# Encoder FFN: four seven-product pairs in the first gate/up block of each later pass, silu as one function, sums in place

## The chip, the cores and the metric

The kernel runs on one core of a Trainium2 chip. The metric is device time in microseconds (us) of one execution. Engines are named as in the profile: PE (matrix), DVE (vector), ACT (scalar), POOL, SP (issues the weight transfers).

## The reference, cut to what matters

A two-layer encoder trunk on 256 rows of width 2048, float32; hidden width of the FFN 5632 (11 blocks of 512). What the change touches is the FFN of both layers:

```python
def swiglu(h, w_gate, w_up, w_down):
    return (jax.nn.silu(h @ w_gate) * (h @ w_up)) @ w_down

for l in range(DEPTH):
    hn = rms_norm(h, mix_norm[l])
    ...
    hn = rms_norm(h, ffn_norm[l])
    h = h + swiglu(hn, ffn_w_gate[l], ffn_w_up[l], ffn_w_down[l])
```

## The kernel before

Every float32 operand is split into a high and a low part, and one product of a 128x128 tile of activations with a 128x512 tile of weights is three matmuls, called h, l and x here: high times high (L301 before, L308 after), high times low of the weights (L302; L309), low of the activations times high (L303; L310).

The hidden columns go in 11 blocks j a layer, 512 gate and 512 up columns each, named f0_j and f1_j by layer. They are taken in passes of blocks 0-1, 2-4, 5-7 and 8-10. After each pass, `stream` computes the down projection of what the pass produced (tiles f0d, f1d), output by output, and adds each output to the residual h on DVE (L283, `residual`). "First block" means blocks 2, 5 and 8, the first of each later pass: three a layer, six in all.

`gate_up` computes one block. It walks over the 16 tiles of 128 rows of the weights as eight pairs p = 0..7. A pair is one 1 MB transfer into `raw` (SP's queue), which holds four 128x512 tiles: gate and up, two rows of tiles each. ACT casts `raw` to `whi`, DVE makes `wlo` = `raw` - `whi` (L324). There are two `wlo` buffers, so `wlo` of pair p cannot begin before PE has read the last of `wlo` of pair p-2. A pair of kind N is eight products, 24 matmuls. A pair of kind S is a seven-product scheme, 21 matmuls, for which DVE forms four sums of the weight tiles (L320 to L322, into `t`), ACT casts them to `thi` (L323) and DVE makes `tlo` (L326); only three of the four plain tiles are then needed, so its `wlo` has 1536 columns. Products of S are P1 to P7, each accumulated in a bank of its own; P6, P7, P4 and P5 use the sums, P1, P2, P3 the plain tiles. Block 0 is plain: N only, with four banks (192 matmuls). The other blocks follow `PAIRS`, a letter for each pair: "NSNSNSNN", 5 x 24 + 3 x 21 = 183 matmuls.

The activation side of a product comes from `x`, or, for P3 of N and most of S, from differences that `make_combos` forms once a layer. A block ends with the gate's silu and the product with up. Eight transposes on PE, which prepare the down projection, lie in every block but the first of a pass.

Inside an engine, instructions run in the order that a scheduler wrote down from priorities. It may therefore let the h matmuls of several products run first, and their l and x later.

Of the kernel before, what the change touches and what calls it, by code (L numbers as in the profile page):

```python
# [72 lines left out]
def trunk(ctx: ExitStack, tc: tile.TileContext, ins, out):  # L73
# [219 lines left out]
    def gate_up(l, j, xs, combos, fx, name, plain, after):
        pattern = "N" * 8 if plain else PAIRS
        bk = [bank("mm", [P, NB], f"{name}_ps{i}") for i in range(4 if plain else 7)]
        uses = {"S": [P1, P2, P3, P6, P7, P4, P5], "N": [0, 1, 2, 3] if plain else [P2, P4, P5, P3]}
# [9 lines left out]
        for p in range(8):  # L306
            raw = wpool.tile([P, 4, NB], F32, tag="raw", name=f"{name}_raw{p}")
# [27 lines left out]
            def w(i):  # L335
                return whi[:, i], wlo[:, i]
# [6 lines left out]
            elif fast:  # L343
# [9 lines left out]
                product(P6, p, sums(1), tw(2), True)
                product(P7, p, sums(3), tw(1), True)
                product(P4, p, x(1, 1), tw(3), True)
                product(P5, p, sums(0), tw(0), True)
            else:
# [666 lines left out]
```

## Time and profile before

| what | value |
|---|---|
| device time, three runs | 2414.62, 2415.92 (median), 2416.74 us |
| profiled execution: its time, its span | 2416.76 us, 2415.0 us |
| PE busy | 2397.6 us, 99% of the span |
| DVE busy, ACT busy | 1744.3 us (72%), 1142.3 us (47%) |
| granted TensorE clock | 1.00 over the FFN blocks (the higher level, 2.4 GHz) |
| bytes moved | 445.50 MB, mean 184 GB/s |

PE is all but never idle: a change of time has to come from fewer matmuls, from the small holes between matmuls, or from new waits of PE. Ends of matmuls are modelled in the profile, so holes are read from their starts. All trace times below are of the profiled execution.

### The profile page before, as it was taken

To read this page: it belongs to the slowest core of one execution; us is meant where nothing else is said; L and a number is where in the kernel's file an instruction comes from. 1 tells how busy PE (TensorE), PEld (TensorE's weight loads), DVE (VectorE), ACT (ScalarE), POOL (GpSimd) and SP (SyncE) were. 2 spreads that over 40 slices of the span, in tenths; PEclk is the share of its full clock that TensorE was granted. 3 is DMA by queue.
4 is the path that set the end of the run, shared out by engine and by line. 5 is a ranking of instruction groups with operands and counts; after the bars stand their busy time and mean duration, and the time that the engine had idled before them with its cause. 6 is when DMAs were issued, how large, how long until landed. Compare 5 with 4: busy or idle time off the path is not lost.

```text
span 2415.0 us, 27558 instructions
## 1 busy us (share of the span) xinstructions
PE 2397.6 (99%) x11212; PEld 1989.3 (82%) x11212; DVE 1744.3 (72%) x1688; ACT 1142.3 (47%) x1056; POOL 54.7 (2%) x63
## 2 busy tenths in 40 slices
PE   8999999999999999999999999999999999999998
PEld 7888888888888888888888888888888888888887
DVE  5658767688678678754768595855878867876884
ACT  5445455455345444454444444454544544544453
...
GB/s 274 161 171 157 174 185 184 197 200 195 192 199 194 196 194 189 209 184 191 165 149 157 157 144 157 153 159 190 191 193 192 196 193 205 186 197 194 205 209 140
DMA packets 63951, 445.50 MB, mean 184 GB/s; under 512 B 6992, under 2 KB 8272, under 8 KB 10576
## 3 DMA queue, kind: packets, MB, share of 16 engines
...
q14 instruction: 39, 0.32, 0.0%
HBM read 441.61 MB, written 2.10 MB: 184 GB/s over the span
## 4 chain that ended last, share of the span: by engine, by line
PE 96%; DVE 2%; DMA 1%; ACT 0%; issue 0%; SPq 0%; ACTq 0%; POOLq 0%; DVEq 0%
PE f_ps L302 12%; PE f_ps L303 12%; PE f_ps L301 12%; PE f1d_ps L166 3%; PE f1d_ps L164 3%; PE f1d_ps L165 3%; PE f0d_ps L166 3%; PE f0d_ps L164 3%; PE f0d_ps L165 3%; PE c_f_ps L165 2%; PE c_f_ps L164 2%; PE c_f_ps L166 2%; PE s_l L765 2%; PE c_i_ps L164 1%; PE c_g_ps L164 1%; PE c_g_ps L166 1%
## 5 line engine op out<-in xcount | busy, mean ns | idle before, releaser
L314 ACT CAST f_whi<-f_raw 128x2048 fp32r<-128x2048 f32 (+1 forms) x176 | 311.2, 1768 | 240.5 <-PE f_ps L303 143.1
L324 DVE TENSOR_TENSOR f_wlo<-f_raw,f_whi 128x2048 fp32r<-128x2048 f32 (+1 forms) x176 | 368.6, 2105 | 43.4 <-PE f_ps L302 32.3
L301 PE MATMUL f_ps<-f_whi,f_x 128*128 128x512 f32 x848 | 331.3, 393 | 0.0
L302 PE MATMUL f_ps<-f_wlo,f_x 128*128 128x512 f32 x848 | 330.2, 389 | 0.9 <-DVE f_wlo L324 0.9
L303 PE MATMUL f_ps<-f_whi,f_x 128*128 128x512 f32 x848 | 330.3, 390 | 0.0
L303 PEld LDWEIGHTS f_ps<-f_whi,f_x 128*128 128x128 f32 x848 | 159.1, 188 | 33.6
L302 PEld LDWEIGHTS f_ps<-f_wlo,f_x 128*128 128x128 f32 x848 | 159.3, 188 | 33.4 <-DVE f_wlo L324 1.3
L301 PEld LDWEIGHTS f_ps<-f_whi,f_x 128*128 128x128 f32 x848 | 159.3, 188 | 32.1
L326 DVE TENSOR_TENSOR f_tlo<-f_t,f_thi 128x2048 fp32r<-128x2048 f32 x60 | 137.3, 2288 | 63.3 <-ACT f_thi L323 63.3
L323 ACT CAST f_thi<-f_t 128x2048 fp32r<-128x2048 f32 x60 | 114.8, 1913 | 134.2 <-DVE f_t L322 108.6
L149 ACT CAST f1d__whi<-f1d__raw 128x2048 fp32r<-128x2048 f32 x44 | 84.4, 1919 | 128.8 <-PE f1d_ps L166 97.5
L150 DVE TENSOR_TENSOR f1d__wlo<-f1d__raw,f1d__whi 128x2048 fp32r<-128x2048 f32 x44 | 100.7, 2289 | 60.6 <-PE f1d_ps L165 32.6
L150 DVE TENSOR_TENSOR f0d__wlo<-f0d__raw,f0d__whi 128x2048 fp32r<-128x2048 f32 x44 | 100.7, 2289 | 59.0 <-PE f0d_ps L165 29.3
L149 ACT CAST f0d__whi<-f0d__raw 128x2048 fp32r<-128x2048 f32 x44 | 84.4, 1918 | 122.1 <-PE f0d_ps L166 91.3
L150 DVE TENSOR_TENSOR c_f_wlo<-c_f_raw,c_f_whi 128x2048 fp32r<-128x2048 f32 x32 | 73.3, 2292 | 72.1 <-PE c_f_ps L165 51.0
L164 PE MATMUL c_f_ps<-c_f_whi,c_x 128*128 128x512 f32 x256 | 101.9, 398 | 0.0
L302 PE MATMUL f_ps<-f_wlo,x_c 128*128 128x512 f32 x260 | 101.1, 389 | 0.0
L303 PE MATMUL f_ps<-f_whi,x_c 128*128 128x512 f32 x260 | 101.1, 389 | 0.0
L301 PE MATMUL f_ps<-f_whi,x_c 128*128 128x512 f32 x260 | 101.1, 389 | 0.0
L165 PE MATMUL c_f_ps<-c_f_wlo,c_x 128*128 128x512 f32 x256 | 99.7, 390 | 0.0
L166 PE MATMUL c_f_ps<-c_f_whi,c_x 128*128 128x512 f32 x256 | 99.7, 389 | 0.0
L149 ACT CAST c_f_whi<-c_f_raw 128x2048 fp32r<-128x2048 f32 x32 | 61.2, 1913 | 76.8 <-PE c_f_ps L166 57.0
...
## 6 DMA issues: line engine op xcount, KB each, us to landing
...
```

The source lines that it names most:

```text
L149: nc.scalar.copy(whi[:, d], raw[:, d])
L150: nc.vector.tensor_tensor(wlo[:, d], raw[:, d], whi[:, d].bitcast(F32), op=ALU.subtract)
L164: nc.tensor.matmul(ps[b], xh[:, k, sl], hi[:, k, :], start=first, stop=False)
L165: nc.tensor.matmul(ps[b], xh[:, k, sl], lo[:, k, :], start=False, stop=False)
L166: nc.tensor.matmul(ps[b], xl[:, k, sl], hi[:, k, :], start=False, stop=end)
L301: nc.tensor.matmul(bk[b], xh, hi, start=b not in seen, stop=False)
L302: nc.tensor.matmul(bk[b], xh, lo, start=False, stop=False)
L303: nc.tensor.matmul(bk[b], xl, hi, start=False, stop=end and final[b] == p)
L314: nc.scalar.copy(whi[:, d], raw[:, d])
L323: nc.scalar.copy(thi, t)
L324: nc.vector.tensor_tensor(wlo[:, d], raw[:, d], whi[:, d].bitcast(F32), op=ALU.subtract)
L326: nc.vector.tensor_tensor(tlo, t, thi.bitcast(F32), op=ALU.subtract)
```

## The change

- `PAIRS` becomes "NNSNSNSN": the three S pairs are 2, 4 and 6 where they were 1, 3 and 5. First blocks follow a new pattern `FIRST`, "SNSNSNSN": four S pairs, 4 x 24 + 4 x 21 = 180 matmuls. Pair 0, with which a block begins, is one of them.
- The sums are formed in place in `raw`, after `wlo` has been made from it (before: into `t`, ahead of `wlo`). The `t` buffer goes. The products of an S pair are called in another order, P1, P6, P7, P2, P4, P5, P3, with the sums in other places.
- `raw` gets four buffers (the pool's three before).
- silu is one ACT function in place of a sigmoid on ACT and a DVE multiply (L411).
- `make_combos` keeps a fifth difference for pairs that are S in one pattern and N in the other, and takes its scratch from the buffer of `thi`.

```diff
-    PAIRS = "NSNSNSNN"
+    PAIRS = "NNSNSNSN"
+    FIRST = "SNSNSNSN"
+    BOTH = "".join(a if a == b else "B" for a, b in zip(PAIRS, FIRST))
...
-        uses = {"S": [P1, P2, P3, P6, P7, P4, P5], "N": [0, 1, 2, 3] if plain else [P2, P4, P5, P3]}
+        uses = {"S": [P1, P6, P7, P2, P4, P5, P3], "N": [0, 1, 2, 3] if plain else [P2, P4, P5, P3]}
...
-            raw = wpool.tile([P, 4, NB], F32, tag="raw", name=f"{name}_raw{p}")
+            raw = wpool.tile([P, 4, NB], F32, tag="raw", name=f"{name}_raw{p}", bufs=RAW_BUFS)
...
                 if fast:
-                    t = fx.tile([P, 4, NB], F32, tag="t", name=f"{name}_t{p}")
                     thi = fx.tile([P, 4, NB], F32R, tag="thi", name=f"{name}_thi{p}")
                     tlo = fx.tile([P, 4, NB], F32R, tag="tlo", name=f"{name}_tlo{p}")
-                    nc.vector.tensor_tensor(t[:, 0:2], raw[:, 0:3:2], raw[:, 3:4].broadcast_to([P, 2, NB]), op=ALU.add)
-                    nc.vector.tensor_tensor(t[:, 2], t[:, 0], raw[:, 2], op=ALU.add)
-                    nc.vector.tensor_tensor(t[:, 3], t[:, 2], raw[:, 1], op=ALU.add)
-                    nc.scalar.copy(thi, t)
                 nc.vector.tensor_tensor(wlo[:, d], raw[:, d], whi[:, d].bitcast(F32), op=ALU.subtract)
                 if fast:
-                    nc.vector.tensor_tensor(tlo, t, thi.bitcast(F32), op=ALU.subtract)
+                    nc.vector.tensor_tensor(raw[:, 2:4], raw[:, 2:4], _ap(raw, 3 * NB, [[-3 * NB, 2], [1, NB]]), op=ALU.add)
+                    nc.vector.tensor_tensor(raw[:, 0], raw[:, 0], raw[:, 2], op=ALU.add)
+                    nc.vector.tensor_tensor(raw[:, 1], raw[:, 0], raw[:, 1], op=ALU.add)
+                    nc.scalar.copy(thi, raw)
+                    nc.vector.tensor_tensor(tlo, raw, thi.bitcast(F32), op=ALU.subtract)
...
-                sg = fx.tile([P, NB], F32, tag="u", name=f"{n}_s{b}", bufs=3)
-                nc.scalar.activation(sg, src, AF.Sigmoid, scale=r(b))
-                nc.vector.scalar_tensor_tensor(out=g, in0=src, scalar=r(b), in1=sg, op0=ALU.mult, op1=ALU.mult)
+                nc.scalar.activation(g, src, AF.Silu, scale=r(b))
...
+                    pattern = None if plain else FIRST if j == blocks[0] else PAIRS
```

What the scheduler makes of it is seen at the start of a first block. On PE, block 5 of layer 0 began with pair 0 as N; the last number in a name is the tile's, banks 4989 to 4995 are P1 to P7, and 4997 and 4998 are `whi` and `wlo` of pair 0:

```order
L301 MATMUL f_5_ps_4990<-f_5_whi_4997,f_x 128x512 [waits Activation_49]
L302 MATMUL f_5_ps_4990<-f_5_wlo_4998,f_x 128x512 [waits DVE_49]
L303 MATMUL f_5_ps_4990<-f_5_whi_4997,f_x 128x512
L301 MATMUL f_5_ps_4990<-f_5_whi_4997,f_x 128x512
L302 MATMUL f_5_ps_4990<-f_5_wlo_4998,f_x 128x512
L303 MATMUL f_5_ps_4990<-f_5_whi_4997,f_x 128x512
```

Now it begins with pair 0 as S (banks 4964 to 4970 are P1 to P7; `whi`, `wlo`, `thi`, `tlo` of pair 0 are 4972, 4973, 4976, 4977; `wlo` of pair 1 is 5007):

```order
L308 MATMUL f_5_ps_4964<-f_5_whi_4972,f_x 128x512 [waits Activation_49]
L309 MATMUL f_5_ps_4964<-f_5_wlo_4973,f_x 128x512 [waits DVE_49]
L310 MATMUL f_5_ps_4964<-f_5_whi_4972,f_x 128x512
L308 MATMUL f_5_ps_4969<-f_5_thi_4976,x_c_2814 128x512 [waits Activation_49]
L308 MATMUL f_5_ps_4970<-f_5_thi_4976,x_c_2814 128x512
L308 MATMUL f_5_ps_4965<-f_5_whi_4972,f_x 128x512
L309 MATMUL f_5_ps_4965<-f_5_wlo_4973,f_x 128x512
L310 MATMUL f_5_ps_4965<-f_5_whi_4972,f_x 128x512
L308 MATMUL f_5_ps_4967<-f_5_thi_4976,f_x 128x512
L308 MATMUL f_5_ps_4968<-f_5_thi_4976,x_c_2814 128x512 [waits DVE_49]
L308 MATMUL f_5_ps_4965<-f_5_whi_5006,f_x 128x512
L309 MATMUL f_5_ps_4965<-f_5_wlo_5007,f_x 128x512 [waits DVE_49]
```

The fourth matmul of the block now reads `thi`, where 24 matmuls in a row read only `whi` and `wlo` of pair 0. Eighteen matmuls into the block, PE reads `tlo` of pair 0, and only behind these eight does P3 read `wlo` of pair 0 for the last time (bank 4966):

```order
L309 MATMUL f_5_ps_4969<-f_5_tlo_4977,x_c_2814 128x512 [waits DVE_49]
L310 MATMUL f_5_ps_4969<-f_5_thi_4976,x_c_2815 128x512
L309 MATMUL f_5_ps_4970<-f_5_tlo_4977,x_c_2814 128x512
L310 MATMUL f_5_ps_4970<-f_5_thi_4976,x_c_2815 128x512
L309 MATMUL f_5_ps_4967<-f_5_tlo_4977,f_x 128x512
L310 MATMUL f_5_ps_4967<-f_5_thi_4976,f_x 128x512
L309 MATMUL f_5_ps_4968<-f_5_tlo_4977,x_c_2814 128x512
L310 MATMUL f_5_ps_4968<-f_5_thi_4976,x_c_2815 128x512
L308 MATMUL f_5_ps_4966<-f_5_whi_4972,x_c_2814 128x512 [waits DVE_49]
L309 MATMUL f_5_ps_4966<-f_5_wlo_4973,x_c_2814 128x512
```

On DVE, the rows ahead of the same block were these (`t` 5031 holds the sums of pair 1, 4957 is the last `wlo` of the down projection, `h_252` the residual):

```order
L150 TENSOR_TENSOR f0d__wlo_4957<-f0d__raw_4955,f0d__whi_4956 128x2048 [waits DVE_49,DMAHW2_49,PE_49,Activation_49]
L320 TENSOR_TENSOR f_5_t_5031<-f_5_raw_5026 128x1024 [waits DMAHW4_49]
L321 TENSOR_TENSOR f_5_t_5031<-f_5_t_5031,f_5_raw_5026 128x512 [waits DVE_49]
L322 TENSOR_TENSOR f_5_t_5031<-f_5_t_5031,f_5_raw_5026 128x512 [waits DVE_49]
L324 TENSOR_TENSOR f_5_wlo_4998<-f_5_raw_4996,f_5_whi_4997 128x2048 [waits DMAHW3_49,PE_49,Activation_49]
L326 TENSOR_TENSOR f_5_tlo_5033<-f_5_t_5031,f_5_thi_5032 128x2048 [waits Activation_49]
L283 TENSOR_TENSOR h_252<-f0d_3_ps_4893,h_252 128x512 [waits PE_49]
L324 TENSOR_TENSOR f_5_wlo_5028<-f_5_raw_5026,f_5_whi_5027 128x1536 [waits PE_49,Activation_49]
L320 TENSOR_TENSOR f_5_t_5096<-f_5_raw_5091 128x1024 [waits DMAHW6_49,DVE_49]
L283 TENSOR_TENSOR h_252<-f0d_3_ps_4894,h_252 128x512 [waits PE_49]
```

They are now (4973 and 4971 are `wlo` and `raw` of pair 0, 5007 and 5037 are `wlo` of pairs 1 and 2):

```order
L151 TENSOR_TENSOR f0d__wlo_4932<-f0d__raw_4930,f0d__whi_4931 128x2048 [waits DVE_49,DMAHW2_49,PE_49,Activation_49]
L325 TENSOR_TENSOR f_5_wlo_4973<-f_5_raw_4971,f_5_whi_4972 128x1536 [waits DVE_49,DMAHW3_49,PE_49,Activation_49]
L328 TENSOR_TENSOR f_5_raw_4971<-f_5_raw_4971 128x1024 [waits DVE_49]
L329 TENSOR_TENSOR f_5_raw_4971<-f_5_raw_4971 128x512 [waits DVE_49]
L330 TENSOR_TENSOR f_5_raw_4971<-f_5_raw_4971 128x512 [waits DVE_49]
L284 TENSOR_TENSOR h_252<-f0d_3_ps_4868,h_252 128x512 [waits PE_49]
L325 TENSOR_TENSOR f_5_wlo_5007<-f_5_raw_5005,f_5_whi_5006 128x2048 [waits DMAHW4_49,PE_49,Activation_49]
L332 TENSOR_TENSOR f_5_tlo_4977<-f_5_raw_4971,f_5_thi_4976 128x2048 [waits Activation_49]
L284 TENSOR_TENSOR h_252<-f0d_3_ps_4869,h_252 128x512 [waits PE_49]
L325 TENSOR_TENSOR f_5_wlo_5037<-f_5_raw_5035,f_5_whi_5036 128x1536 [waits DMAHW5_49,PE_49,Activation_49]
```

Before, the sums of pair 1 stood ahead of `wlo` of pair 0; now `wlo` of pair 0 stands first, its sums follow, and `tlo` of pair 0 comes behind the residual's add and `wlo` of pair 1. All six first blocks have these orders. SP's and POOL's orders are as before. ACT has four table loads (ACT_TABLE_LOAD) where it had two: before, one for an exponential at the kernel's start (L108) and one at the first sigmoid of layer 0; now one at the start, at the first silu of layer 0, at the first sigmoid of stage c (layer 1's mixer), and at the first silu of layer 1.

## Rows read from the trace of the kernel before

**Rows 1.** Part 1 of the page: busy time of each engine.

```profile
PE 2397.6 (99%) x11212; PEld 1989.3 (82%) x11212; DVE 1744.3 (72%) x1688; ACT 1142.3 (47%) x1056; POOL 54.7 (2%) x63
```

**Rows 2.** Waits of PE: producer, total us, times, longest.

```profile
PE f_ps L302 <- DVE f_tlo L326: 0.9, 3, 0.5
```

**Rows 3.** Timeline of PE, start of layer 0, block 5 (start, duration).

```profile
681.64 0.39 PE L301 MATMUL f_ps<-f_whi,f_x 128*128 128x512 f32 x1
681.87 0.39 PE L302 MATMUL f_ps<-f_wlo,f_x 128*128 128x512 f32 x1
```

**Rows 4.** Window of a first block (length; busy PE, PEld, DVE, ACT, POOL).

```profile
681.64:723.12 41.48, 41.48 (x185) 34.35 (x183) 32.19 (x25) 20.60 (x13) 0.00 (x0) 1.00 0.55 191
```

**Rows 5.** Windows, the fourteen other blocks, and their sum.

```profile
530.12:572.57 42.45, 42.45 (x192) 35.13 (x191) 36.73 (x35) 21.28 (x16) 0.00 (x0) 1.00 0.56 198
572.57:615.38 42.81, 42.81 (x192) 34.97 (x191) 37.08 (x33) 23.08 (x17) 0.00 (x0) 1.00 0.56 198
723.12:766.76 43.64, 42.78 (x193) 35.06 (x191) 38.05 (x36) 21.48 (x17) 0.00 (x0) 1.00 0.57 204
...
1867.46:1911.13 43.67, 43.04 (x192) 34.98 (x191) 36.66 (x34) 21.06 (x16) 0.00 (x0) 1.00 0.53 192
...
2104.13:2147.34 43.21, 42.97 (x193) 34.97 (x191) 37.09 (x33) 23.09 (x17) 0.00 (x0) 1.00 0.56 195
...
sum 599.39, PE 597.66 PEld 490.65 DVE 510.26 ACT 308.29 POOL 0.00; mean PE 42.69 PEld 35.05 DVE 36.45 ACT 22.02 POOL 0.00
```

**Rows 6.** Timeline of PE, block 6 of layer 0.

```profile
730.94 0.50 PE L302 MATMUL f_ps<-f_wlo,f_x 128*128 128x512 f32 x1 [0.86 <-DVE f_wlo L324]
```

**Rows 7.** Chain that ended last, block 6 of layer 0.

```profile
709.81 6.66 DMA f_raw<-in_w_gu
```

**Rows 8.** Timeline of PE in block 4, layer 0: first tlo.

```profile
593.02 0.40 PE L302 MATMUL f_ps<-f_wlo,f_x 128*128 128x512 f32 x1
593.28 0.50 PE L302 MATMUL f_ps<-f_tlo,x_c 128*128 128x512 f32 x1
593.61 0.40 PE L303 MATMUL f_ps<-f_thi,x_c 128*128 128x512 f32 x1
```

**Rows 9.** Timeline of DVE around the start of block 5, layer 0.

```profile
673.00 1.22 DVE L320 TENSOR_TENSOR f_t<-f_raw 128x1024 f32<-128x1024 f32 x1
674.25 0.69 DVE L321 TENSOR_TENSOR f_t<-f_t,f_raw 128x512 f32<-128x512 f32 x1
674.98 0.69 DVE L322 TENSOR_TENSOR f_t<-f_t,f_raw 128x512 f32<-128x512 f32 x1
676.23 2.29 DVE L324 TENSOR_TENSOR f_wlo<-f_raw,f_whi 128x2048 fp32r<-128x2048 f32 x1 [0.56 <-PE f0d_ps L165]
678.44 2.29 DVE L326 TENSOR_TENSOR f_tlo<-f_t,f_thi 128x2048 fp32r<-128x2048 f32 x1
681.16 0.69 DVE L283 TENSOR_TENSOR h<-f0d_ps,h 128x512 f32<-128x512 f32 x1 [0.44 <-PE f0d_ps L166]
681.77 1.75 DVE L324 TENSOR_TENSOR f_wlo<-f_raw,f_whi 128x1536 fp32r<-128x1536 f32 x1
...
687.11 2.29 DVE L324 TENSOR_TENSOR f_wlo<-f_raw,f_whi 128x2048 fp32r<-128x2048 f32 x1 [0.43 <-PE f_ps L302]
```

**Rows 10.** Timeline of ACT there.

```profile
675.70 1.91 ACT L323 CAST f_thi<-f_t 128x2048 fp32r<-128x2048 f32 x1 [2.82 <-DVE f_t L322]
```

**Rows 11.** Timeline of PE: last reader of the first wlo.

```profile
686.63 0.39 PE L302 MATMUL f_ps<-f_wlo,x_c 128*128 128x512 f32 x1
```

**Rows 12.** A line of DVE, by shape (count, busy, mean ns).

```profile
L411 DVE SCALAR_TENSOR_TENSOR f_g<-f_g,f_rstd,f_s 128x512 f32<-128x512 f32 x40 | 29.8, 746 | 1.5 <-ACT f_s L410 1.3
```

**Rows 13.** Timeline of ACT: end of block 0, layer 0; stage c.

```profile
399.10 1.28 ACT L410 ACT_TABLE_LOAD   x1
400.39 1.27 ACT L410 ACTIVATE f_s<-f_ps,f_rstd 128x512 f32<-128x512 f32 x2
...
1116.33 0.69 ACT L723 ACTIVATE q<-c_q_ps,c_rstd 128x512 f32<-128x512 f32 x1 [2.84 <-PE c_q_ps L166]
```

More of the change, by code (lines that the diff above doesn't have):

```diff
@@ L45 @@
 ALIGN = 128
+RAW_BUFS = 4
 WLO_BUFS = 2
@@ L135, in stream @@
         for i, kg, nb, ps in [(i, kg, nb, ps) for i, kg in enumerate(kgs) for nb, ps in zip(nbs, pss)]:
-            raw = wpool.tile([P, KG, NB], F32, tag="raw", name=f"{name}_raw{i}")
+            raw = wpool.tile([P, KG, NB], F32, tag="raw", name=f"{name}_raw{i}", bufs=RAW_BUFS)
             whi = wpool.tile([P, KG, NB], F32R, tag="whi", name=f"{name}_whi{i}")
@@ L290, in trunk, with gate_up @@
     P1, P2, P3, P4, P5, P6, P7 = range(7)
-    PAIRS = "NSNSNSNN"
-    def gate_up(l, j, xs, combos, fx, name, plain, after):
-        pattern = "N" * 8 if plain else PAIRS
+    PAIRS = "NNSNSNSN"
+    FIRST = "SNSNSNSN"
+    BOTH = "".join(a if a == b else "B" for a, b in zip(PAIRS, FIRST))
+    def gate_up(l, j, xs, combos, fx, name, pattern, after):
+        plain = pattern is None
+        pattern = pattern or "N" * 8
         bk = [bank("mm", [P, NB], f"{name}_ps{i}") for i in range(4 if plain else 7)]
-        uses = {"S": [P1, P2, P3, P6, P7, P4, P5], "N": [0, 1, 2, 3] if plain else [P2, P4, P5, P3]}
+        uses = {"S": [P1, P6, P7, P2, P4, P5, P3], "N": [0, 1, 2, 3] if plain else [P2, P4, P5, P3]}
         seen, final = set(), {b: p for p in range(8) for b in uses[pattern[p]]}
@@ L350, in gate_up @@
                 product(P1, p, x(0, 0), w(0), True)
+                product(P6, p, sums(1), tw(0), True)
+                product(P7, p, sums(3), tw(2), True)
                 product(P2, p, x(1, 0), w(1), True)
+                product(P4, p, x(1, 1), tw(1), True)
+                product(P5, p, sums(0), tw(3), True)
                 product(P3, p, sums(2), w(2), True)
[L353 to L356, printed above, removed]
             else:
@@ L368, in gate_up, with make_combos @@
         return bk
-    def make_combos(xs, cp, combos, name):
+    def make_combos(xs, fx, combos, name):
         for p in range(8):
@@ L375, in make_combos @@
             k0 = p % 2 * 2
-            n = 4 if PAIRS[p] == "S" else 2
-            c = [cp.tile([P, n, P], F32R, tag=f"c{p}{i}", name=f"{name}_c{p}{i}", bufs=1) for i in range(2)]
-            parts = tmp.tile([P, 2, n, P], F32, tag="hh", name=f"{name}_cp{p}", bufs=2)
+            n = {"N": 2, "S": 4, "B": 5}[BOTH[p]]
+            c = [fx.tile([P, n, P], F32R, tag=f"c{p}{i}", name=f"{name}_c{p}{i}", bufs=1) for i in range(2)]
+            parts = fx.tile([P, 2, n, P], F32, tag="thi", name=f"{name}_cp{p}")
             def x(k, b):
                 return xt[:, :, k0 + k, b * P:(b + 1) * P]
-            if n == 4:
+            if n > 2:
                 nc.vector.tensor_tensor(parts[:, :, 0], x(0, 1), x(1, 1), op=ALU.subtract)
@@ L388, in make_combos @@
                 nc.vector.tensor_tensor(parts[:, :, 3], x(0, 0), x(0, 1), op=ALU.subtract)
+                if n == 5:
+                    nc.vector.tensor_tensor(parts[:, :, 4], x(1, 0), x(1, 1), op=ALU.subtract)
             else:
@@ L430, in after @@
                             halves.get(len(halves.makers) - (2 if p == 1 else 1))
-                        if not plain and p == PAIRS.rindex("S"):
+                        if not plain and p == pattern.rindex("S"):
                             with tc.high_priority(offset=2 * AHEAD):
@@ L437, in after @@
                                 early["u"] = u1, u2, u3
-                    bk = gate_up(l, j, xs, combos, fx, n, plain, after)
+                    bk = gate_up(l, j, xs, combos, fx, n, pattern, after)
                     hh = tmp.tile([P, 2, NB], F32, tag="hh", name=f"{n}_hh", bufs=2)
```

5 lines of the change are left out of this document (3 added, 2 removed).

## The prediction

> **What bounds the kernel now.** I read the page first, and in it the busy shares: PE is busy 99% of the span, DVE 72%, ACT 47% [rows 1]. So time can be lost or won only at PE, and I went on to what PE waits for. Of all the FFN's waits for sums the list names three, 0.9 us together [rows 2]; small near-misses do not reach that list, so I took the spacing of matmul starts instead. Undisturbed it is 0.23 us (681.64, 681.87) [rows 3]. A first block is nothing but this: its 183 matmuls take 41.48 us [rows 4], 0.2267 each, with no hole at all, and all six first blocks have that length. The other fourteen sum to 599.39 us [rows 5], and have three sorts: about 42.45 (eight transposes and small holes above 41.48), about 42.81 to 42.86 (the third of a pass), and three above that: 43.64, 43.67 and 43.21.
>
> The third sort comes from waits. In block 6 of layer 0 PE waits 0.86 us for `wlo` [rows 6], and the chain goes back from there to a weight transfer of 6.66 us, begun late for want of a `raw` buffer [rows 7]. The second sort comes from ties at `tlo`: in block 4 the matmul that first reads it starts 0.26 us after the one before it (0.04 late), and the next one 0.33 later (0.11 late) [rows 8]. So a wait of w costs PE about w + 0.11 us; a tie costs some 0.14 us, and 42.83 is 42.45 and two to three ties.
>
> **What the change takes away.** Six first blocks lose three matmuls each: 18 x 0.2267 = 4.1 us. No other block's number changes.
>
> **What it adds in a first block.** I chain the new order from durations before, T being the block's first matmul (681.64 in block 5).
> - DVE's `wlo` of the first pair waits for a buffer that the down projection frees at T - 5.41 (676.23, ended by PE) [rows 9]. The down projection is untouched, so the new `wlo`, 1.75 us long as the 1536-column one at 681.77 [rows 9], starts there too and ends at T - 3.66.
> - Before, the sums were made while DVE waited (673.00 to 675.67). Now they come behind it: from 673.00 to 675.67 they took 2.67 us [rows 9], so they end at T - 0.99. ACT's cast to `thi` is 1.91 us and starts 0.03 us after the sums (675.70) [rows 10]: ready at T + 0.95. PE wants it as its fourth matmul, at T + 0.68. With 0.03 to 0.05 us for the handover the wait is 0.32, and with the 0.11 behind it 0.43 us.
> - On DVE follow the residual's add (681.16, next start at T + 0.13) and `wlo` of pair 1 (2.20 from start to next start, as 676.23 to 678.44), so `tlo` runs from T + 2.33 to T + 4.62 [rows 9]. PE is there after 18 matmuls and the wait above: 18 x 0.2267 + 0.43 = 4.51. Wait 0.15, cost 0.26 us.
> - `wlo` of pair 2 needs the buffer of pair 0's, which P3 now reads last, 27 matmuls on: T + 0.69 (waits so far) + 27 x 0.2267 = 6.81. From the last reader's start to DVE's start it took 0.48 us (686.63 to 687.11) [rows 9, 11]: 7.29, `wlo` to 9.04, sums to 11.73, `wlo` of pair 3 (2.29) to 14.02. PE reaches pair 3 after 57 matmuls and 0.69 at T + 13.61. Wait 0.45, cost 0.56 us.
> - The later S pairs (4 and 6) are one period further, and come out within 0.1 us of a tie each; I take 0.14 for both together.
>
> Sum of a first block: 0.43 + 0.26 + 0.56 + 0.14 = 1.39 us of waits against 0.68 saved, +0.71; six of them **+4.3 us**. The lower end is no wait at all, -4.1; the upper, all waits twice as long, 6 x (2.78 - 0.68) = +12.6. I take the worked value, since each link is a row of the same place and buffer.
>
> **The fourteen other blocks.** The same number of matmuls and of sums, but sums now after `wlo`, so `thi` and `tlo` come later in DVE's row. Chained in the same way for pair 2, from a block's start: PE's last read of pair 0's `wlo` is 23 matmuls on, 5.21, so `wlo` begins at 5.69 and its sums end at 10.1, `thi` at 12.05. PE wants `thi` after 52 matmuls and four of the eight transposes (half of 42.45 - 41.48 less the holes, some 0.36), 12.15: in time. `wlo` of pair 3 needs pair 1's buffer, read last 47 matmuls on: 11.13; `tlo` of pair 2 comes behind it, 13.33 to 15.62. PE wants it after 67 matmuls and those 0.36 at 15.55: 0.07 late, a tie like block 4's. The next S pairs repeat this within 0.1 us. So I give all fourteen block 4's length: 14 x 42.83 = 599.6 against 599.39, **+0.2 us**. In this two things cancel. The 42.45 blocks get slower by 0.38, because the block ahead of them no longer leaves DVE time in hand: a first block kept DVE busy 32.2 of 41.48 us [rows 4] and gets a fourth S pair (2.67 of sums and 2.29 of `tlo`), some 90% of its new length. And the 43.64, 43.67 and 43.21 fall by 0.4 to 0.8, because the fourth `raw` buffer lets their transfers go out one pair sooner. As `raw` is now held until `tlo` is made, the buffer may only make up for that; then those three keep their 2.0 us above 42.83. Low end: no ties, 14 x 42.45 = 594.3, -5.1. High end: each tie doubled, +6.
>
> **At no cost.** The DVE multiply of silu goes (746 ns each, 40 in the row of this shape [rows 12], 44 in the program); it stands at a block's end on DVE, while PE is in the next block's first pair, whose `wlo` are made already, so it gives back DVE time that nothing waits for; if that cover were gone it would be worth up to 1.5 us a block, and part of it is the low end above. The fifth difference is one more short DVE row in the plain block, where PE has no S pair to wait for. The two added table loads: 1.28 us of ACT [rows 13]. Stage c's falls where ACT waits 2.84 us for PE [rows 13]; layer 1's falls at the first silu, as the one before did at the first sigmoid, without a wait of PE in the list. If neither were hidden, 2 x 1.28 = 2.6 us.
>
> Here a rule speaks against the change. In this trace the next activation starts at 400.39, when the load (399.10 and 1.28) has just ended [rows 13]. The Trainium skill, "ScalarE: Activation LUTs", section "What ACT_TABLE_LOAD costs", says that a drain of some 1.38 us comes on top, 2.66 us for every switch to another set. No drain shows in these rows. By the page two switches would be 5.3 us of ACT, and the time 2425.8 if PE had to wait for all of it; by the rows it is 2420.5 if hidden, 2423.1 if not.
>
> **Sum.** +4.3 + 0.2 = +4.5 us. The profiled execution took 2416.76, so it would take 2421.3; it lies 0.84 above the median of the runs, 2415.92, so for a median I say **2420.5 us**. A measurement tells about 0.2%, or 4.8 us, from no change: 2411.1 to 2420.7 counts as the same. Only the waits decide: the saving is 0.17%.
>
> **Rivals.**
> - *The first blocks do not wait (faster side).* DVE gets to `wlo` and the sums of pair 0 sooner, or the order leaves PE enough other h matmuls. For it: before, `wlo` of pair 0 was ended by a buffer, not by DVE's load, and DVE loses 1.5 us of silu a block. Against: that buffer is freed by PE in the down projection, at T - 5.41, and wlo, sums and cast are 6.36 us in a row. It decides if `thi` is there by T + 0.68. Then 2415.9 - 4.1 + 0.2 = 2412.0; with no ties elsewhere either, 2406.7. Chance 0.15.
> - *The ties of the fourteen fall well.* A tie is 0.04 us of lateness, and the silu's DVE time may be enough to lift all of them. Then 2420.5 - 5.3 = 2415.2. Chance 0.18.
> - *The ties of the fourteen double*, because PE's order takes h of P6, P7, P4, P5 early and leaves DVE two rows behind: 2426.3. Chance 0.13.
> - *The table loads show*: 2423.1, chance 0.04.
> - My forecast: 0.48, with its own range 2417 to 2424. The last 0.02 is for a cause that no row shows.
>
> **How the numbers follow.** Faster by over 0.2% needs the first rival and something of the second, since 2412.0 alone is just within: 0.10 of its 0.15, and the 0.02 of an unseen cause. Slower: half of my forecast, which lies at the edge (0.24), doubled ties (0.13), loads (0.04): 0.41. Same: the other half (0.24), the second rival (0.18) and the rest of the first (0.05): 0.47. The range must reach down past 2412.0 and up past the doubled ties: 2411 to 2427 leaves out the first rival's 0.10 and the little beyond the doubled ties, under 0.2.
>
> **What would show it.** Right: the six first blocks about 42.2 us long, with PE waits for `thi` of pair 0 (0.3), `tlo` of pair 0 (0.15) and `wlo` of pair 3 (0.45) in each; the other fourteen within 42.4 to 42.9, none at 43.6; ACT loads with no PE wait behind them. Wrong: first blocks of 40.8 us (no waits), or of 43 and more; `wlo` of pair 0 starting far from T - 5.41; or the fourteen moving by more than 5 us together.

## The result, and the profile after

The changed kernel takes **2432.5 us** (median of six runs, 2431.8 to 2433.8), the kernel before 2416.0: a ratio of 1.007, interval 1.0061 to 1.008. It is 16.5 us slower. The forecast of 2420.5 had the right direction; the loss is well over three times the 4.5 us forecast and lies outside the range.

Part 1 of the page of the changed kernel, to be held against [rows 1]:

```profile
PE 2407.7 (99%) x11194; PEld 1982.1 (82%) x11194; DVE 1754.9 (72%) x1674; ACT 1151.0 (47%) x1064; POOL 53.9 (2%) x63
```

PE is busy ten us longer with 18 matmuls fewer, and the span grew by 16.7 (2415.0 to 2431.7). The busy time does not say what the ten us are: a matmul is drawn 0.39 us long where starts lie 0.23 apart [rows 3], so short holes between matmuls count as busy, just as slower matmuls do. The list of PE's waits, the counterpart of [rows 2], names the places of the longer waits (producer, total, times, longest):

```profile
PE f_tp L207 <- DVE h L903: 2.9, 1, 2.9
PE f_tp L207 <- DVE h L284: 2.9, 1, 2.9
PE f_ps L309 <- DVE f_wlo L325: 1.5, 6, 0.3
PE f_ps L308 <- ACT f_thi L331: 1.3, 6, 0.2
```

The last two rows are two of the first blocks' waits, six times each, as forecast (the third, for `tlo`, is too short for the list). The first two were not forecast at all: 2.9 us at the last transpose before each layer's plain block, where PE waits for the residual h. The timeline of PE there, in layer 0 (start, duration, idle before):

```profile
359.85 0.30 PE L207 MATMUL f_tp<-ident,h 128*128 128x128 f32 x1 [2.85 <-DVE h L284]
359.90 0.48 PE L308 MATMUL f_ps<-f_whi,f_x 128*128 128x512 f32 x1
...
361.24 0.63 PE L309 MATMUL f_ps<-f_wlo,f_x 128*128 128x512 f32 x1
361.67 0.63 PE L310 MATMUL f_ps<-f_whi,f_x 128*128 128x512 f32 x1
```

and windows over the wait and over the 4 us behind it (length; busy time of PE, PEld, DVE, ACT, POOL; granted clock; DMA share, GB/s):

```profile
356.80:359.85 3.05, 0.20 (x2) 0.04 (x2) 3.05 (x4) 2.54 (x3) 0.00 (x0) 1.00 0.06 24
359.85:364.00 4.15, 4.15 (x12) 3.29 (x13) 3.69 (x11) 1.63 (x5) 0.71 (x1) 0.59 0.74 253
364.00:368.00 4.00, 4.00 (x19) 3.28 (x19) 2.28 (x4) 1.33 (x2) 0.00 (x0) 1.00 0.00 0
```

Behind the wait the matmuls stand 0.43 us apart in place of 0.23, and the granted clock falls to a mean of 0.59: most of the stretch ran at the lower level, 1.2 GHz, after PE had stood still for 2.85 us. It is the higher level again in the next window. In layer 1 the wait is 2.91 us, and the clock over the 4.2 us behind it 0.61. The Trainium skill, "TensorE: Matmul & The Clock Gate", section "Wait — 56ns, not 53.3ns?", gives 426.7 ns from start to start for 512 columns on a cold array; these rows agree (361.67 less 361.24). For a warm one it gives 215.7 ns; there this kernel's rows show 226.7, and the rows decide.

So a plain block that took 44.49 us takes 46.07 (layer 0) and 45.94 (layer 1), on top of the wait. What DVE did in that time:

```profile
356.16 0.69 DVE L401 TENSOR_TENSOR x_cp<-x_cp 128x512 f32<-128x512 f32 x1
356.81 2.29 DVE L325 TENSOR_TENSOR f_wlo<-f_raw,f_whi 128x2048 fp32r<-128x2048 f32 x1
359.01 1.28 DVE L284 TENSOR_TENSOR h<-eout_ps,h 128x512 f32<-128x512 f32 x2
```

In the kernel before the same rows of DVE, read the same way:

```profile
356.02 0.42 DVE L391 TENSOR_TENSOR x_cp<-f_x 128x256 f32<-128x256 f32 x1
356.39 0.69 DVE L283 TENSOR_TENSOR h<-eout_ps,h 128x512 f32<-128x512 f32 x1
357.00 2.28 DVE L324 TENSOR_TENSOR f_wlo<-f_raw,f_whi 128x2048 fp32r<-128x2048 f32 x1
```

and PE's transpose came right after that add, without a wait in the list:

```profile
357.14 0.33 PE L206 MATMUL f_tp<-ident,h 128*128 128x128 f32 x1
```

The first of the last two adds of h stood ahead of the plain block's second `wlo`; now both stand behind it. h waits for the 2.29 us of `wlo`, and PE's last transpose waits for h. DVE's rows at layer 1's start show the same (`wlo` at 1702.34, the adds of h at 1704.55).

The first blocks, the counterpart of [rows 4], and the fourteen others with their sum, the counterpart of [rows 5]:

```profile
688.14:730.64 42.50, 42.04 (x182) 33.40 (x180) 37.06 (x29) 22.19 (x15) 0.00 (x0) 1.00 0.58 209
```

```profile
535.87:578.84 42.97, 42.97 (x193) 34.75 (x191) 37.53 (x32) 22.34 (x16) 0.00 (x0) 1.00 0.53 194
578.84:621.84 43.00, 43.00 (x193) 34.75 (x191) 37.53 (x32) 22.33 (x16) 0.00 (x0) 1.00 0.53 197
730.64:773.62 42.98, 42.98 (x193) 34.75 (x191) 37.53 (x32) 22.34 (x16) 0.00 (x0) 1.00 0.54 194
...
1881.44:1924.38 42.94, 42.94 (x192) 34.75 (x191) 37.52 (x32) 22.32 (x16) 0.00 (x0) 1.00 0.53 193
...
sum 601.50, PE 601.50 PEld 486.48 DVE 522.32 ACT 312.63 POOL 0.00; mean PE 42.96 PEld 34.75 DVE 37.31 ACT 22.33 POOL 0.00
```

Taken from the starts of matmuls, block by block, the 16.7 us are: the two FFN starts 8.1 (later first matmuls 2.7 and 2.4, slower plain blocks 3.0), the six first blocks 5.9 (254.8 against 248.9), the fourteen others 2.1, and 0.6 in the down projections and behind the last block.

The waits in a first block follow the forecast's chain almost link for link. DVE's rows ahead of block 5 of layer 0, whose first matmul is T = 688.14:

```profile
682.73 1.76 DVE L325 TENSOR_TENSOR f_wlo<-f_raw,f_whi 128x1536 fp32r<-128x1536 f32 x1 [3.15 <-PE f0d_ps L166]
684.52 1.22 DVE L328 TENSOR_TENSOR f_raw<-f_raw 128x1024 f32<-128x1024 f32 x1
...
686.50 0.69 DVE L330 TENSOR_TENSOR f_raw<-f_raw 128x512 f32<-128x512 f32 x1
...
688.27 2.28 DVE L325 TENSOR_TENSOR f_wlo<-f_raw,f_whi 128x2048 fp32r<-128x2048 f32 x1
690.47 2.29 DVE L332 TENSOR_TENSOR f_tlo<-f_raw,f_thi 128x2048 fp32r<-128x2048 f32 x1
...
695.46 1.76 DVE L325 TENSOR_TENSOR f_wlo<-f_raw,f_whi 128x1536 fp32r<-128x1536 f32 x1 [2.11 <-issue]
...
699.85 3.95 DVE L325 TENSOR_TENSOR f_wlo<-f_raw,f_whi 128x2048 fp32r<-128x2048 f32 x2
```

`wlo` of pair 0 starts at 682.73, T - 5.41 to the hundredth; `tlo` ends at 692.76, T + 4.62; `wlo` of pair 2 starts at T + 7.32 (forecast 7.29). PE's rows at the two larger waits:

```profile
688.59 0.39 PE L310 MATMUL f_ps<-f_whi,f_x 128*128 128x512 f32 x1
689.20 0.73 PE L308 MATMUL f_ps<-f_thi,x_c 128*128 128x512 f32 x2 [0.22 <-ACT f_thi L331]
...
702.19 0.50 PE L309 MATMUL f_ps<-f_wlo,f_x 128*128 128x512 f32 x1 [0.25 <-DVE f_wlo L325]
```

The fourth matmul starts 0.61 after the third, 0.38 late (forecast 0.32). The first reader of pair 3's `wlo` starts 0.64 after the matmul ahead of it (701.55), 0.41 late (forecast 0.45).

### The profile page after: what moved, and what is told of

Read it like the earlier page. It is cut to its first block, busy times and chain, and to the rows that moved or that the text cites. A ratio compares the mean times of both kernels' runs of the same rounds, so it can differ in the third digit from the quotient of the medians.

```text
span 2431.7 us, 27501 instructions
## 1 busy us (share of the span) xinstructions
PE 2407.7 (99%) x11194; PEld 1982.1 (82%) x11194; DVE 1754.9 (72%) x1674; ACT 1151.0 (47%) x1064; POOL 53.9 (2%) x63
## 4 chain that ended last, share of the span: by engine, by line
PE 96%; DVE 2%; ACT 1%; issue 0%; DMA 0%; ACTq 0%; POOLq 0%; DVEq 0%
PE f_ps L309 13%; PE f_ps L310 13%; PE f_ps L308 12%; PE f0d_ps L165 3%; PE f1d_ps L165 3%; PE f0d_ps L166 3%; PE f1d_ps L166 3%; PE f0d_ps L167 3%; PE f1d_ps L167 3%; PE c_f_ps L166 2%; PE c_f_ps L165 2%; PE c_f_ps L167 2%; PE s_l L773 2%; PE c_g_ps L165 1%; PE c_g_ps L167 1%; PE c_i_ps L167 1%
## 5 line engine op out<-in xcount | busy, mean ns | idle before, releaser
L309 PE MATMUL f_ps<-f_wlo,f_x 128*128 128x512 f32 x824 | 322.8, 392 | 1.5 <-DVE f_wlo L325 1.5
L308 PE MATMUL f_ps<-f_whi,f_x 128*128 128x512 f32 x824 | 323.5, 395 | 0.0
L310 PE MATMUL f_ps<-f_whi,f_x 128*128 128x512 f32 x824 | 322.2, 391 | 0.0
L331 ACT CAST f_thi<-f_raw 128x2048 fp32r<-128x2048 f32 x66 | 126.0, 1910 | 208.2 <-DVE f_raw L330 208.2
L310 PEld LDWEIGHTS f_ps<-f_whi,f_x 128*128 128x128 f32 x824 | 155.4, 189 | 32.9
L308 PEld LDWEIGHTS f_ps<-f_whi,f_x 128*128 128x128 f32 x824 | 155.5, 189 | 31.7
L332 DVE TENSOR_TENSOR f_tlo<-f_raw,f_thi 128x2048 fp32r<-128x2048 f32 x66 | 150.9, 2286 | 12.3 <-ACT f_thi L331 12.3
```

The source lines that it names most:

```text
L308: nc.tensor.matmul(bk[b], xh, hi, start=b not in seen, stop=False)
L309: nc.tensor.matmul(bk[b], xh, lo, start=False, stop=False)
L310: nc.tensor.matmul(bk[b], xl, hi, start=False, stop=end and final[b] == p)
L331: nc.scalar.copy(thi, raw)
L332: nc.vector.tensor_tensor(tlo, raw, thi.bitcast(F32), op=ALU.subtract)
```

## The experiments

All times are medians beside runs of the kernel before on the same chip, which took 2415.5 to 2415.9 us in each group. Block lengths in the table run from a block's first matmul to its last plus one step, summed over the six first blocks, the fourteen others and the two plain ones. Where a first block and the one after it overlap on PE, the first two are given together (the kernel before: 848.3).

| kernel | us | six first | fourteen others | two plain |
|---|---|---|---|---|
| before | 2416.0 | 248.9 | 599.4 | 89.0 |
| changed | 2432.5 | 254.8 | 601.5 | 92.0 |
| e1 | 2430.0 | 255.2 | 602.4 | 90.2 |
| e2 | 2425.4 | 254.7 | 602.0 | 89.0 |
| e3 | 2423.3 | 252.9 | 601.7 | 89.0 |
| e4 | 2421.7 | 244.8 | 608.6 | 89.0 |
| e5 | 2411.7 | 843.4 | together | 89.0 |
| e6 | 2412.7 | 248.9 | 594.9 | 89.0 |
| e7 | 2411.8 | 248.9 | 594.2 | 89.0 |
| e8 | 2425.5 | 252.5 | 603.9 | 89.0 |
| e9 | 2407.5 | 244.8 | 594.2 | 89.0 |
| e10 | 2436.1 | 252.5 | 616.0 | 89.0 |
| e11 | 2411.3 | 842.9 | together | 89.0 |
| e12 | 2427.7 | 252.0 | 600.2 | 89.5 |
| e13 | 2425.5 | 254.6 | 601.8 | 89.0 |
| e14 | 2454.4 | 244.8 | 637.3 | 89.0 |

**The FFN starts: e1 and e2.** The theory is that DVE's row order at the start costs 8.6 us in all. e1 moves h alone, in layer 0 alone:

```diff
-        residual(nb, pd)
+        with tc.high_priority(offset=2 * AHEAD if nb == 3 else 0):
+            residual(nb, pd)
```

> The changed kernel with one thing moved: at the start of layer 0's FFN, DVE's last two adds to the residual h stand ahead of the second weight pair's wlo instead of behind it; layer 1's start is left alone. Theory (half of the lost time is PE waiting, and then running at the lower clock, because h stands behind a wlo of 2.29 us): PE's 2.9 us wait at layer 0's first transpose goes, block f0_0 falls from 46.07 to about 44.5 us, the one at layer 1's start stays at 2.9 us; in all 2432.5 - 2.7 - 1.6 = 2428.2 us. Rival (the wait is of the sums or differences behind, and only moves): the wait shows at another tile and the time stays within 1 us of 2432.5.

It took 2430.0 us, interval 1.0043 to 1.0073. The waits of PE, by the list:

```profile
PE f_tp L207 <- DVE h L904: 2.9, 1, 2.9
...
PE f_tp L207 <- DVE h L284: 0.5, 1, 0.5
```

Layer 0's wait fell to 0.5 us and its plain block to 44.50; layer 1's, untouched, is still 2.9. The first matmul of f0_0 comes 2.4 us sooner. By the spans (2428.6 against 2431.7) the gain is 3.1 us (2.5 by the medians, 4.3 forecast) of the 4.0 that start and plain block gave; some 1 us was lost again in the blocks behind (f0_3 43.35, f0_5 42.85). The rival, that the wait only moves and the time stays, is out. e2 undoes the edit from which the order came, the one scratch buffer of `make_combos`:

```diff
-            parts = fx.tile([P, 2, n, P], F32, tag="thi", name=f"{name}_cp{p}")
+            parts = tmp.tile([P, 2, n, P], F32, tag="hh", name=f"{name}_cp{p}", bufs=2)
```

> The changed kernel with make_combos' scratch back in the two buffers it had before (the changed kernel has one). Theory (with one buffer the scheduler puts the differences of pair 2 and the wlo of pair 1 ahead of the last add to h, in both layers): both 2.9 us waits at the FFN starts and both stretches at the lower clock go, 2 x 4.3 = 8.6 us, 2423.9 us; the six first blocks stay at 42.45 and the fourteen others at 42.95. Rival (the fifth difference alone makes DVE late there): the waits stay, 2432.5 us.

2425.4 us, interval 1.0025 to 1.0055 (2423.9 forecast); both starts are as before (first matmul of f0_0 at 357.60, plain blocks 44.49 and 44.46), and the other columns of the table stayed. One add of h is ahead of `wlo` again:

```profile
356.76 0.69 DVE L284 TENSOR_TENSOR h<-eout_ps,h 128x512 f32<-128x512 f32 x1
357.37 2.28 DVE L325 TENSOR_TENSOR f_wlo<-f_raw,f_whi 128x2048 fp32r<-128x2048 f32 x1
```

So the rival, that the fifth difference alone does it, is out: the fifth difference is still made here. The one buffer let the scheduler put the work in another order, and the new order put h behind `wlo`.

**The first blocks and the fourteen others: e3, e4, e8, e9.** e3 takes the fourth pair away (`FIRST = PAIRS`, on top of e2).

> As the run with two scratch buffers, and the first blocks follow the pattern of the others (three seven-product pairs, starting with an eight-product pair; 183 matmuls). Theory (the waits of the first blocks come from beginning with a seven-product pair, about 0.49 for thi of pair 0, 0.17 for its tlo, 0.52 for wlo of pair 3): first blocks 41.48 + 3 ties of 0.15 = 41.9 us against 42.45, -3.3 us, so 2420.6 us; the fourteen others stay at 42.95. Rival (the fourth seven-product pair leaves DVE behind and it is this that makes the ties of the blocks after it): those fourteen fall to 42.45 to 42.8 too, 2414 to 2418 us.

2423.3 us, interval 1.0021 to 1.0044. First blocks lost 1.8 us though they have 18 matmuls more; the others stayed (601.7). So less than the theory said comes from beginning with a fourth S pair: the first blocks are 42.15 us each, where 41.9 were expected. The rival about the blocks after is out. e4 puts a fourth pair into the kernel before, with the sums ahead:

```diff
     PAIRS = "NSNSNSNN"
+    FIRST = "NSNSNSNS"
...
```

> The kernel before with one part of the change in another form: first blocks have a fourth seven-product pair as their last pair (NSNSNSNS), sums made ahead of wlo into a buffer of their own, in the old order of products; silu, buffers and pattern of the other blocks as before. Theory (what costs is that a first block begins with a seven-product pair and that the sums come behind wlo, not the fourth pair itself): first blocks 180 x 0.2267 = 40.8 us with at most one tie of 0.15, 2416.0 - 4.1 + up to 0.9 = 2411.9 to 2412.8 us. Rival (a fourth seven-product pair is more than DVE can carry in a first block): waits of 0.7 us or more in each first block or the block after it, 2416 us or more.

2421.7 us, interval 1.0016 to 1.0036: in the first blocks the theory is right to the hundredth, 40.80 us each, in all the rival is nearer: the block after each loses 2.3 us. PE's waits and, around the end of f0_2 (529.02), DVE's rows:

```profile
PE f_ps L305 <- DVE f_wlo L327: 10.1, 6, 1.7
```

```profile
529.39 0.68 DVE L443 TENSOR_TENSOR f_u<-f_ps,f_u 128x512 f32<-128x512 f32 x1
...
533.71 1.41 DVE L420 SCALAR_TENSOR_TENSOR f_hh<-f_hh,f_rstd,f_g 128x512 f32<-128x512 f32 x2
...
535.63 3.95 DVE L327 TENSOR_TENSOR f_wlo<-f_raw,f_whi 128x1536 fp32r<-128x1536 f32 x2
```

The rows of the block's end (sums of banks, silu, gate) fill DVE up to 535.1, and the next block's second `wlo` (the first of the two in the last row) comes behind them. e8 has the changed kernel with two scratch buffers, and the old pattern in all blocks:

> The changed kernel with two scratch buffers, and the pattern of before (NSNSNSNN) for first and other blocks alike; sums in place behind wlo, product order, silu and four raw buffers as changed. Theory (the fourteen other blocks went from 42.45 or 42.83 to 42.95 because the sums come behind wlo, so each tlo ties): they stay at 42.9 to 43.0, first blocks about 41.9 to 42.15, 2422 to 2424 us, as the run with three seven-product pairs. Rival (it is the shifted pattern): they fall to 42.45 to 42.83 and first blocks to 41.48, 2413 to 2417 us.

2425.5 us, interval 1.0025 to 1.0055; the first blocks are 42.1 us each, and the fourteen others even rose to 603.9 (43.1 each). So the shifted pattern is not what costs. e9 then undoes the sums in place, on top of e2:

```diff
+                    t = fx.tile([P, 4, NB], F32, tag="t", name=f"{name}_t{p}")
+                    nc.vector.tensor_tensor(t[:, 0:2], raw[:, 0:3:2], raw[:, 3:4].broadcast_to([P, 2, NB]), op=ALU.add)
+                    nc.vector.tensor_tensor(t[:, 2], t[:, 0], raw[:, 2], op=ALU.add)
+                    nc.vector.tensor_tensor(t[:, 3], t[:, 2], raw[:, 1], op=ALU.add)
+                    nc.scalar.copy(thi, t)
                 nc.vector.tensor_tensor(wlo[:, d], raw[:, d], whi[:, d].bitcast(F32), op=ALU.subtract)
...
-                    nc.vector.tensor_tensor(raw[:, 2:4], raw[:, 2:4], _ap(raw, 3 * NB, [[-3 * NB, 2], [1, NB]]), op=ALU.add)
-                    nc.vector.tensor_tensor(raw[:, 0], raw[:, 0], raw[:, 2], op=ALU.add)
-                    nc.vector.tensor_tensor(raw[:, 1], raw[:, 0], raw[:, 1], op=ALU.add)
-                    nc.scalar.copy(thi, raw)
...
```

> The run with two scratch buffers (2425.4 us) with one part undone: the four sums go into a buffer of their own ahead of wlo, as in the kernel before; patterns, product order, silu and four raw buffers as changed. Theory (what is left of the loss is the sums in place, which put 2.67 us of DVE and the 1.9 us cast behind wlo's wait for its buffer): no wait for thi or tlo, first blocks 40.8 to 41.2 us, the fourteen others 42.45, that is 2415.8 - 4.1 - 5.2 + up to 2 = 2406.5 to 2409 us. Rival (beginning with a seven-product pair, or the shifted pattern, costs by itself): first blocks 41.5 us or more, others over 42.6, 2412 us or more.

2407.5 us, interval 0.9955 to 0.9979: the fastest of all, 18 us under e2 and 8.0 under the kernel before beside it (2415.5), as the theory had it. Two windows of it (columns as above), a first block and the one after:

```profile
488.56:529.36 40.80, 40.80 (x181) 33.78 (x180) 34.51 (x28) 22.07 (x15) 0.00 (x0) 1.00 0.59 197
529.36:571.82 42.46, 42.46 (x193) 35.13 (x191) 37.13 (x32) 22.15 (x17) 0.00 (x0) 1.00 0.58 198
```

All six first blocks are 180 x 0.2267 = 40.80 us, all others 42.43 to 42.45. DVE ahead of block 5, whose first matmul is at 680.54:

```profile
671.90 1.22 DVE L326 TENSOR_TENSOR f_t<-f_raw 128x1024 f32<-128x1024 f32 x1
...
673.88 0.69 DVE L328 TENSOR_TENSOR f_t<-f_t,f_raw 128x512 f32<-128x512 f32 x1
675.50 1.76 DVE L330 TENSOR_TENSOR f_wlo<-f_raw,f_whi 128x1536 fp32r<-128x1536 f32 x1 [0.92 <-PE f0d_ps L167]
```

The sums lie ahead of DVE's wait for the `wlo` buffer, as in [rows 9].

**What about the sums in place: e10, e12, e13.** e10 is that part alone, in the kernel before.

> The kernel before with one part alone: the sums in place in raw, behind wlo, and the buffer t gone; old pattern, old order of products, sigmoid and multiply, three raw buffers. Theory (it is this part that makes the ties): the fourteen other blocks rise from 42.45 or 42.83 to 43 us or more, first blocks to 41.9 or more, +8 to +14 us, 2424 to 2430 us. Rival (the order of the products is what the ties come from): within 2 us of 2415.8.

2436.1 us, interval 1.0068 to 1.0099, +20.7: more than the theory's upper end. Beside the ties (blocks of 43.8) there is a wait that had not been named:

```profile
PE f_ps L301 <- ACT f_whi L314: 7.6, 12, 1.9
```

`raw` is now held until `tlo` is made, and with three buffers the next weights come late: in this run's list ACT's `whi` waits for a weight transfer 62 times, 166.1 us together (before: 11 times, 9.8, and DVE's sums 12 times, 20.0). e8, with four buffers (and silu and the new product order), has no such wait; the fourth buffer alone was not added to e10. e12 gives e2 a third `wlo` buffer (and takes back the fourth of `raw`, for room: `WLO_BUFS = 3`, `RAW_BUFS = 3`).

> The run with two scratch buffers (2425.4 us; sums in place, behind wlo) with three wlo buffers in place of two, and three raw buffers in place of four, for room. Theory (the sums in place are late because wlo, ahead of them now, waits until PE has read the wlo of two pairs before; the wait is passed on to sums, thi and tlo): with a third buffer that wait goes, the waits for thi, tlo and wlo go with it, first blocks 40.8 to 41.2 us, others 42.45 to 42.6, 2407.5 to 2411 us, but for late transfers of up to 2 us from the missing raw buffer. Rival (the chain wlo, sums, cast, tlo is too long by itself, or raw is held too long): first blocks 42 us or more, others 42.9 or more, 2422 us or more.

2427.7 us, interval 1.003 to 1.0064. The theory's numbers did not come; the rival's did, to within 0.03 us: first blocks 42.0, others 42.87. DVE's rows at block 5 (first matmul 688.30):

```profile
679.13 1.76 DVE L325 TENSOR_TENSOR f_wlo<-f_raw,f_whi 128x1536 fp32r<-128x1536 f32 x1 [2.72 <-ACT f_whi L321]
...
685.00 2.29 DVE L325 TENSOR_TENSOR f_wlo<-f_raw,f_whi 128x2048 fp32r<-128x2048 f32 x1 [1.40 <-ACT f_whi L321]
```

`wlo` now waits for ACT's `whi`, which has three buffers and itself waits for PE: the wait went one step up the chain. Nothing in the FFN waits for a weight transfer in this run, so it is not `raw` held too long. The parts outside the FFN also lost (the first matmul of f0_0 comes at 362.06), so the total says nothing more. e13 separates the place in DVE's row from the place in memory: e9 with the sums in their own buffer, kept behind `wlo` on DVE, which leaves `raw` free sooner.

```diff
+                    with tc.issue_after(wi):
+                        nc.vector.tensor_tensor(t[:, 0:2], raw[:, 0:3:2], raw[:, 3:4].broadcast_to([P, 2, NB]), op=ALU.add)
...
```

Here `wi` is the instruction that makes `wlo`.

> The run with the sums ahead (2407.5 us), with one thing moved: the sums still go into a buffer of their own, but the first of them may not stand ahead of the pair's wlo on DVE, so DVE's row is wlo, sums, tlo as in the changed kernel. Theory (it is the place behind wlo in DVE's row, and wlo's wait for its buffer, that costs; holding raw longer costs nothing): first blocks about 42.4 us, others about 42.95, 2425 us, as the run with two scratch buffers. Rival (it is raw being held until tlo is made): as with the sums ahead, 40.8 and 42.45, 2407.5 us.

2425.5 us, interval 1.0025 to 1.0055, the theory: e2 again, in all three columns, though PE's waits in block 5 are now for `thi` and `tlo` of pair 0 (0.26 and 0.18 us) and `thi` of pair 2 (0.31). DVE ahead of block 5 (first matmul 684.31):

```profile
678.90 1.76 DVE L326 TENSOR_TENSOR f_wlo<-f_raw,f_whi 128x1536 fp32r<-128x1536 f32 x1 [3.15 <-PE f0d_ps L166]
680.58 1.22 DVE L329 TENSOR_TENSOR f_t<-f_raw 128x1024 f32<-128x1024 f32 x1
```

With `wlo` at T - 5.41 and the sums behind it, the loss is there without anything in place. `raw` is still held somewhat longer than in e9, until the sums are made, but in e13, e2 and the changed kernel nothing in the FFN waits for a weight transfer. It is the order, not the memory.

**The parts forecast at nothing: e6 and e7.**

> The kernel before with four raw buffers in place of three, and nothing else but a smaller scratch for DMA descriptors to make room. Theory (the three long blocks of before, 43.64, 43.67 and 43.21 us, waited for transfers that a buffer held up): they fall to 42.45, 42.83 and 42.85, sum -2.4 us, 2413.4 us; nothing else moves. Rival (the transfers were late for another reason): 2415.8 us, the three stay. Rival 2 (transfers that go out sooner collide with those of the down projection): new waits elsewhere, over 2416.5 us.

> The kernel before with silu as one ACT function (two more table loads) and nothing else. Theory (the loads of 1.28 us lie where ACT waits, and the DVE multiply saved lies where nothing waits): 2415.8 us within 1 us, four table loads and no wait of PE behind one. Rival (a switch of tables costs 2.66 us and PE waits for it): PE waits behind both, up to +5.3 us, 2421 us. Rival 2 (DVE's 1.5 us a block take the ties away): the 42.85 blocks fall to 42.45, 2413.5 us.

Four raw buffers alone: 2412.7 us, interval 0.9978 to 0.9997. The three long blocks fell as expected, to 42.4 to 42.6, and the ties of f0_4, f0_7 and the like went too, down to 42.43, which had not been expected. (The smaller scratch for DMA descriptors is part of the change too, though the list of changes does not name it, and it is in e4, e5 and e11; no run has it alone.) silu alone: 2411.8 us, interval 0.9973 to 0.9992, with all fourteen at 42.43 to 42.45. Rival 2 of e7 is right, and the waits of the long blocks went too: the DVE time is worth 4 us, more than the 2.3 that rival 2 gave it. Of the table loads, ACT's rows at the first silu of the changed kernel, the counterpart of [rows 13]:

```profile
402.71 1.28 ACT L418 ACT_TABLE_LOAD   x1
404.01 1.27 ACT L418 ACTIVATE f_g<-f_ps,f_rstd 128x512 f32<-128x512 f32 x2
```

The function starts 0.02 us after the load; none of PE's waits stands behind a load. The Trainium skill, "ScalarE: Activation LUTs", section "What ACT_TABLE_LOAD costs", adds a drain of some 1.38 us to each switch; the load itself agrees (1.28). No drain is seen here, and in e7 no wait of PE stands behind the two added switches.

**Better versions: e5, e11, e14.** e5 has `FIRST = "NSNSNSSN"` in e4.

> The kernel before, with the fourth seven-product pair of first blocks as pair 6 of 0 to 7 (NSNSNSSN), so that an eight-product pair still ends the block; sums ahead of wlo as before. In the run with the fourth pair at the end first blocks were 40.80 us and each block after one lost 2.3 us at its second wlo, which DVE made late behind the block-end sums. Theory (the loss is that the last pair's tlo and the block-end operations fall together, not DVE's load): first blocks 40.8 to 41.0 us, the blocks after them back to 42.45 or 42.85, 2415.8 - 4.1 + up to 1.5 = 2411.7 to 2413.2 us. Rival (a fourth pair in any place leaves DVE late in the next block): the blocks after keep 1 us or more of it each, 2418 us or more.

2411.7 us, interval 0.9974 to 0.9993: the theory's time, but by another sum. The wait for the second `wlo` that e4 had is gone from PE's list. Yet a first block and the block after it take 83.87 to 83.95 us together, as much as in the kernel before where no transfer was late (41.48 + 42.45 = 83.93): what the first block saves, the block after it loses in ties. The gain lies in the two pairs that had been long (85.12 and 85.15 before, -2.5 us) and in the third blocks of the passes (257.4 to 255.1, -2.3). So the hit of the number is luck in part. e11 adds silu to it.

> The kernel before with the fourth seven-product pair of first blocks as pair 6 (2411.7 us alone) and silu as one function (2411.8 us alone). Theory (the two gains are of different kinds, 18 matmuls and DVE time at a block's end, and add up but for the 0.2 us a pass that the fourth pair costs in the blocks after it): 2415.8 - 4.1 - 4.0 = 2407.7 us, down to 2406.5 if silu also takes that 0.2 away. Rival (both took away the same late transfers, 2.0 us, which can be won once): 2409.7 us.

2411.3 us, interval 0.9974 to 0.9992. The gains did not add up, and the rival is right in kind: what e5 had gained, in the long pairs and the third blocks, silu alone had taken away too (e7), and it can be won once. The first two blocks of a pass are 83.64 to 83.75 us, so some 0.2 of the 0.68 saved is kept; one block (f0_7, 43.67) has a new wait of 1.0 us at a transpose, whose cause is open, and the time is over the rival's 2409.7. e14 gives e9 four such pairs in all twenty blocks (`PAIRS = "SNSNSNSN"`).

> The run with the sums ahead (2407.5 us) with four seven-product pairs in all 20 blocks that are not plain (SNSNSNSN), not in six. Theory (with sums ahead of wlo DVE has time: it was busy 34.5 to 37.1 us of a block of 40.8 to 42.5; a fourth pair adds 2.67 for sums, 2.29 for tlo, takes 0.54 from wlo, to some 40 of 41.8): each of the fourteen loses 0.68 us, -9.5, 2398 us. Rival (with DVE busy 96% of the block its row falls behind and PE waits for wlo or tlo): the fourteen stay above 42.4 us, 2407 us or more.

2454.4 us, interval 1.0141 to 1.0175; blocks 4, 7 and 10 take some 50 us.

```profile
PE f_6T_tp L207 <- DVE f_6T_x L211: 6.6, 2, 3.3
```

```profile
574.05 2.28 DVE L330 TENSOR_TENSOR f_wlo<-f_raw,f_whi 128x2048 fp32r<-128x2048 f32 x1
...
576.85 0.68 DVE L211 TENSOR_TENSOR f_3T_x<-f_3T_tp,f_3T_x 128x512 fp32r<-128x512 f32 x1
```

```profile
572.00:616.00 44.00, 39.03 (x159) 30.92 (x160) 34.69 (x28) 20.47 (x14) 0.00 (x0) 0.92 0.48 168
```

PE waits 3.3 us in each of these six blocks, at the transposes, for what DVE makes of them (L211), and the clock's mean over the 44 us falls to 0.92: behind the wait twelve matmuls stand 0.43 us apart. In block 4 that L211 comes behind the end of the block before, a `wlo` and two sums, and DVE is busy without a hole from 569.7 to 577.5. Over the 44 us it is busy only 34.7, so its sum of work alone is not the bound; its row does fall behind at the block's start. The rival had the side right, and waits for `wlo` or `tlo` are not what PE shows. No run moves L211 ahead.

## Why the prediction was wrong, point by point

**What bounds the kernel, and what the change takes away.** Right: 18 matmuls, and PE is all that counts.

**What it adds in a first block.** The mechanism is shown: the chain holds link by link, and e9 and e13 turn the waits off and on by the one order it rests on. The sum was 1.39 us of waits a block and measured some 1.66 (254.76 / 6 = 42.46 less 40.80); so +5.9 in place of +4.3. The three named waits came to some 1.18 us (1.25 forecast). Mis-sized are the two later ties, taken as 0.14 together, which cost 0.12 to 0.13 each, and delays of 0.01 us at single matmuls behind a wait, taken as nothing, which add up to some 0.25.

**The fourteen other blocks.** Forecast +0.2, measured +2.1. Right that all take one pattern of ties (42.93 to 43.03) and that the blocks of 43.6 go. Mis-sized by 0.13 us a block: three ties in each, where two to three were taken. The rival "ties fall well" was no idle one: e7 and e9 show it, but only with the sums ahead.

**At no cost.** This is the step that failed, and in both directions. "The fifth difference is one more short DVE row in the plain block, where PE has no S pair to wait for": what counted was not its 0.4 us but the scratch buffer that goes with it, which moved an add of h behind a `wlo` in each layer. That is 8.1 us of the span's 16.7, and about 3 us of it come after the waits, at the lower clock. e2 shows it: without that one edit the time is 2425.4, 7.1 less and inside the range, and what is then left of the loss is the forecast's own waits and ties, 8.4 us by the table where 4.5 were worked out. It could have been read in the changed kernel's order, in DVE's rows ahead of the plain block; the prediction looked at that order only at the starts of the first blocks. And "DVE time that nothing waits for": silu alone gains 4.0 us in the kernel before (e7), and with it the ties and the late `wlo` of block 6 are gone. What it is worth inside the changed kernel no run shows, since none there goes without it. The fourth `raw` buffer, counted at the 2.0 us of the three long blocks, gains 3.1 us alone (e6).

**The rivals.** None of them named the start of the FFN. No wait of PE stands behind a table load. The direction was forecast for a reason that holds (the waits of the first blocks), not by luck. "What would show it" gave first blocks of 42.2 (42.46 came), and the fourteen within 42.4 to 42.9 (42.93 to 43.03).
